# Moving two-input elementwise work of a hybrid decoder kernel from GpSimd to VectorE and ScalarE

## The chip, the cores and the metric

The kernel runs on one core of a Trainium2 chip. The metric is the device time of one execution in microseconds (us). Before the change it is 800.0 us, the median of three runs (799.88 to 800.56).

A core has TensorE for matmuls (PE in the profile; PEld is its loading of weights), VectorE (DVE) and ScalarE (ACT) for elementwise work, GpSimd (POOL), which also does elementwise work, and SyncE (SP), which issues the DMAs here. Each engine works through its own queue in order and waits on semaphores for the others.

## What is computed

Two layers of a decoder with model width 1024 on 256 tokens. Each layer normalises its input, makes one combined projection and feeds three token mixers from it: retention with a rotary embedding (`ret`), attention with a forget gate (`fox`) and an RWKV-7 recurrence (`rwkv`). Their outputs are projected, weighted by sigmoid gates, summed and projected again; then comes a SwiGLU feed-forward part. Cut to what the change touches:

```python
for l in range(DEPTH):
    proj = _rmsnorm(x, mix_norm[l]) @ w_in[l]
    ret_c, fox_c, rwkv_c, gate_c = jnp.split(proj, splits, axis=-1)
    ...
    merged = gates[0] * (y_ret @ p_ret[l]) + gates[1] * (y_fox @ p_fox[l]) + gates[2] * (y_rwkv @ p_rwkv[l])
    x = x + merged @ w_out[l]
    ...
def _rwkv7_branch(cols, mu, ...):
    prev = jnp.pad(cols[:, :-1], ((0, 0), (1, 0), (0, 0)))
    cols = cols + (prev - cols) * mu          # the token mix
    r, k, v, xw, xa, xg = jnp.split(cols, ...)
    ...
    k = k * (1.0 + (a - 1.0) * k_a)           # k2 in the kernel
    y = _rwkv7_scan(r, decay, k, v, -kk, kk * a)
def _rotary(t, pos):
    return jnp.concatenate([t1 * cos - t2 * sin, t1 * sin + t2 * cos], axis=-1)
```

Everything is float32.

## The kernel before

**Layout.** Channels lie on the 128 partitions and the 256 tokens along the free axis. A tile of two channel groups is 128 x 512 elements; most elementwise instructions here have that shape, or half of it (128x256, or 64x512 for half of the partitions).

**Matmuls.** A float32 product is made from three matmuls of rounded parts: weight high by input high, weight high by input low, weight low by input high (L290, L293, L294, in `mm3`; `mm3n` with L437 to L439 has the operands the other way round). The parts of the weights are made on the fly in `_piece`: SyncE loads a raw piece (L263), ScalarE rounds it to `whi` (L273, 128x1024), VectorE subtracts to get `wlo` (L274, 128x1024). Some pieces are made ahead (`AHEAD = 3`, four buffers of each part). So VectorE and ScalarE feed TensorE with weights all the time and do all other elementwise work between the pieces. Inputs of matmuls are split in the same manner by `split`: ScalarE makes `hi` (L376), VectorE or GpSimd makes `lo` (L377).

**Order of the work.** `mixers` starts with the first projections and then runs generators side by side: `gemms` (projections and gates, the long supply of matmuls), `rwkv`, `fox` and `ret`. Each yields a cost out of the table `PACE`, and the one with the smallest sum goes next. That sets the order in which the instructions are written; the order on each engine is then made by a scheduler at build time, which works with priorities (`early`, `high_priority`) and its own estimates of durations, so that an instruction can stand elsewhere in its queue than in the text. On the chip the queues are fixed.

**Buffers.** Most 128x512 tiles come out of one pool, `t2`, with 13 buffers under one tag; a new tile waits until one is free.

**The places that the change touches**, in the order of a layer:

- `rwkv_in` (from L622): the token mix. For each of four pairs of channel groups (r, k, v, and wg for the low-rank inputs) VectorE scales the projection into `pj` (L642), with one column more at the front that GpSimd sets to zero (L640). GpSimd subtracts neighbours into `dd` (L644), and VectorE makes dd * mu + pj (L633, two of 128x256). The multiply-adds of one pair are written after the scaling of the next.
- `rwkv` (from L655): k2 = (scaled a) * k on GpSimd (L730), feeding the second pair of `bk` writes (L732) and rkk (L745), which feeds the matmul pb (L748); two copies of v into `rav` on GpSimd (L735); rs = r-part * decay on GpSimd (L740), read much later (L894); nn = masked part of gg on GpSimd (L786), read by matmuls at L842. Between gg (L764) and L842 stands the inversion of small triangles: gg goes to DRAM and back by DMA into `lt`, a serial solve on VectorE follows (L821, L823), the result goes through DRAM again into `tb`, is transposed (L837) and meets nn at L842.
- `ret` (from L1103): four DMAs make the swapped rows `sw` of the rotary embedding (L1112), two load the cosine and sine tables `cs` (L1114, L1115). GpSimd multiplies qk by the cosine, in place (L1116), VectorE multiplies sw by the sine (L1117) and adds (L1118); the sum feeds the scores psc (L1138), which VectorE masks (L1140, L1141).
- `gemms` (from L529): the merge. With ps the projected branch, VectorE makes (g + 1) * ps (L567) and the sum m += g (L569) runs on GpSimd for all four column groups of the second branch and for the first group (c = 0) of the third; the other three run on VectorE. Of the finished m, hi is made on ScalarE and lo (L377) on GpSimd for c = 0, on VectorE for the others. The output projection, which comes next on TensorE, needs hi and lo of c = 0 first.
- `fox` is not changed; its reduction for the softmax (L1057), its scaling (L1064) and the transposes px (L1068) run beside the `rwkv` steps above.

Of the kernel before, what the change touches and what calls it, by code (L numbers as in the profile page):

```python
# [8 lines left out]
F32 = mybir.dt.float32  # L9
# [4 lines left out]
ALU = mybir.AluOpType  # L14
AX = mybir.AxisListType

P = 128
# [133 lines left out]
class Kernel:  # L151
# [377 lines left out]
    def gemms(self, l, xs, rstd, rn):  # L529
        nc, d = self.nc, self.d  # L530
        fx = []
        self.need = None
        for _ in self.fox_in(l, xs, rn, fx):
            yield PACE["gemms0"]
        self.start.append(("fox", self.fox(l, fx)))
        rt = []
        for _ in self.ret_in(l, xs, rstd, rn, rt):
            yield PACE["gemms1"]
        self.start.append(("ret", self.ret(l, rt)))
        yield PACE["gemms2"]  # L540
        gates = {}
        for b in (0, 1, 2):
            for c in range(4):
                gen = self.gemm_pair(xs)
                while True:
                    try:
                        next(gen)
                    except StopIteration as e:
                        ps = e.value
                        break  # L550
                    yield PACE["gemms3"]
                g = gates[b, c] = self.big.tile([P, 2, T], F32, tag="gate", bufs=8, name=self.nm("gate"))
                nc.vector.tensor_tensor(out=g, in0=ps, in1=self.b2(rstd), op=ALU.mult)  # L553
                nc.scalar.activation(g, g, AF.Tanh, scale=0.5)
                yield PACE["gemms3"]
            if b == 0:
                continue
            for bb in ((0, 1) if b == 1 else (2,)):
                self.need = ("ret", "fox", "rwkv")[bb]
                yield PACE["gemms4"]  # L560
                self.need = None
                y = [(self.y[bb][0][:, k, :], self.y[bb][1][:, k, :]) for k in range(2)]
                for c in range(4):
                    ps = self.run(self.gemm_pair(y))
                    g, m = gates[bb, c], gates[0, c]
                    with self.early("hp_merge"):
                        nc.vector.scalar_tensor_tensor(out=g, in0=g, scalar=1.0, in1=ps, op0=ALU.add, op1=ALU.mult)  # L567
                        if bb:
                            (nc.vector if bb == 2 and c >= 1 else nc.gpsimd).tensor_tensor(out=m, in0=m, in1=g, op=ALU.add)  # L569
                    if bb == 2:  # L570
                        with self.early("hp_turn"):
                            hi, lo = self.split(self.t2, m, [P, 2, T], ("t2", "t2"), nc.gpsimd if c < 1 else nc.vector)
                        self.mx.extend((hi[:, i, :], lo[:, i, :]) for i in range(2))
                    elif c % 2:
                        yield PACE["gemms5"]
# [46 lines left out]
    def rwkv_in(self, l, xs, rstd, first):  # L622
# [5 lines left out]
        wg = self.t512("wg")  # L628
        dst = [r, k, v, wg]

        def mix(j, pj, dd):
            for i in range(2):
                nc.vector.scalar_tensor_tensor(out=dst[j][:, i, :], in0=dd[:, i, :], scalar=self.prm(l, "mu", 2 * j + i),  # L633
                                               in1=pj[:, i, 1:], op0=ALU.mult, op1=ALU.add)

        last = None
        for j in range(4):
            ps = first[j] if j < len(first) else self.run(self.gemm_pair(xs))
            pj = self.big.tile([P, 2, T + 1], F32, tag="pj", bufs=2, name=self.nm("pj"))
            nc.gpsimd.memset(pj[:, :, 0:1], 0.0)  # L640
            for o, p in self.parts(ps):
                nc.vector.tensor_tensor(out=pj[:, o, 1:], in0=p, in1=self.bs(rstd, o), op=ALU.mult)  # L642
            dd = self.t512("dd")
            nc.gpsimd.tensor_tensor(out=dd, in0=pj[:, :, 0:T], in1=pj[:, :, 1:], op=ALU.subtract)  # L644
            if last:
                mix(*last)
            last = j, pj, dd
        mix(*last)
        return r, k, v, wg, rav

    @staticmethod
# [3 lines left out]
    def rwkv(self, l, rw):  # L655
# [71 lines left out]
        k2 = self.t512("k2")  # L727
        for i in range(2):
            nc.scalar.activation(k2[:, i, :], ta[:, i, :], AF.Identity, scale=hb[:, 4 + i:5 + i], bias=hb[:, 6 + i:7 + i])
        nc.gpsimd.tensor_tensor(out=k2, in0=k2, in1=k, op=ALU.mult)  # L730
        for h in range(2):
            nc.vector.tensor_tensor(out=bk[hs[h], :, (1 - h) * C:(2 - h) * C], in0=ch(k2)[hs[h]], in1=ch(pinv)[hs[h]], op=ALU.mult)  # L732
        nc.vector.tensor_tensor(out=rav[:, :, 0:C], in0=ch(r), in1=pp[:, :, 1:], op=ALU.mult)
        for h in range(2):
            nc.gpsimd.tensor_copy(rav[hs[h], :, (2 - h) * C:(3 - h) * C], ch(v)[hs[h]])  # L735
        rs = self.t2.tile([P, 2, NC, C], F32, tag="t2", name=self.nm("rs"))
        r4 = rav.rearrange("p (a c) x -> p a c x", a=2)
        p4 = pp.rearrange("p (a c) x -> p a c x", a=2)
        pend = p4[:, :, 0:NC - 1, C:C + 1].broadcast_to([P, 2, NC - 1, C])
        nc.gpsimd.tensor_tensor(out=rs[:, :, 1:, :], in0=r4[:, :, 1:, 0:C], in1=pend, op=ALU.mult)  # L740
        yield PACE["rwkv5"]

        rkk = self.t512("rkk")
# [39 lines left out]
        nc.gpsimd.memset(tb, 0.0)  # L783
        nn = self.t2.tile([P, NP, C], F32, tag="t2", name=self.nm("nn"))
        for h in range(2):
            nc.gpsimd.tensor_tensor(out=nn[hs[h]], in0=gg[hs[h], h::2, 2 * C:],  # L786
                                    in1=c["nmask"][hs[h]].unsqueeze(1).broadcast_to([64, NP, C]), op=ALU.mult)

        idn = c["ident"]
# [313 lines left out]
    def ret(self, l, rt):  # L1103
# [9 lines left out]
        cs = self.t512("cs")  # L1113
        nc.sync.dma_start(cs[:, 0, :], self.dc("cos"))  # L1114
        nc.sync.dma_start(cs[:, 1, :], self.dc("sin"))  # L1115
        nc.gpsimd.tensor_tensor(out=qk, in0=qk, in1=b4(cs[:, 0, :]), op=ALU.mult)  # L1116
        nc.vector.tensor_tensor(out=sw, in0=sw, in1=b4(cs[:, 1, :]), op=ALU.mult)  # L1117
        nc.vector.tensor_tensor(out=qk, in0=qk, in1=sw, op=ALU.add)  # L1118
        yield PACE["ret0"]
# [77 lines left out]
```

## Time and profile before

| | |
|---|---|
| median of three runs | 800.0 us (799.88 to 800.56) |
| the profiled execution | 800.76 us, of which the span of its instructions is 799.0 |
| busy: PE, PEld | 783.6 us (98%), 762.5 us (95%) |
| busy: DVE, ACT, POOL | 576.2 us (72%), 397.1 us (50%), 61.6 us (8%) |
| instructions on DVE, ACT, POOL | 900, 543, 83 |
| granted TensorE clock | 1.000 |
| HBM | 137 MB read, 173 GB/s over the span |

How to read it: a row of an instruction has the line in the kernel, the engine, the operation, the tile written and those read, shapes, and how many there are. Behind the bar come the busy time in us and the mean of one in ns, then the idle time of the engine just before and what ended it. Rows of a timeline begin with the start and the length in us; in brackets stands the idle time of the engine before the row and what ended it. Since TensorE is busy nearly all the time, idle time on another engine says little; what counts are the waits of TensorE. Spans on GpSimd are rougher than the others.

### The profile page before, as it was taken

The page shows a single profiled execution, that of the slowest core. Times are in us where ns is not written, and L with a number is a line of the kernel's source. Part 1 is how long each engine was busy: PE and PEld are TensorE (multiplying, and loading weights), DVE is VectorE, ACT ScalarE, POOL GpSimd, SP SyncE. Part 2 cuts the span into 40 slices and gives each one's busy share as a digit, 9 for nine tenths or more (in the row PEclk, how much of TensorE's full clock was granted, in tenths as well). Part 3 has the DMA queues.
Part 4 walks back from the last instruction along what each step waited for, and adds up shares of the span by engine and source line. Part 5 has one row for each costly group of instructions (what it writes and reads, how often), then busy time and mean ns, then how long its engine had stood idle before and what let it go on. Part 6 is the DMA issues. An engine that isn't in the chain of part 4 may idle for free.

```text
span 799.0 us, 16543 instructions
## 1 busy us (share of the span) xinstructions
PE 783.6 (98%) x7018; PEld 762.5 (95%) x7018; DVE 576.2 (72%) x900; ACT 397.1 (50%) x543; POOL 61.6 (8%) x83
## 2 busy tenths in 40 slices
PE   8999899999999999999999999999999999999998
PEld 6999899999999999999998988999999999999997
DVE  5897979597867666656678798877878666666453
ACT  6367445535645444445444764554456545444331
POOL 3201210031000000000023030101110000000000
PEclk9999999999999999999999999999999999999999
DMA  8565524335454554556554553452445454555650
GB/s 308 208 226 167 170 80 169 140 114 205 161 208 167 203 205 172 191 184 211 200 188 175 197 172 106 162 174 106 142 176 190 180 201 174 206 202 164 211 190 27
DMA packets 27802, 140.42 MB, mean 176 GB/s; under 512 B 7600, under 2 KB 9168, under 8 KB 12496
## 3 DMA queue, kind: packets, MB, share of 16 engines
q1 hardware_dynamic: 27728, 139.36, 50.2%
q8 instruction: 55, 0.90, 0.5%
q14 instruction: 19, 0.16, 0.1%
HBM read 136.97 MB, written 1.33 MB: 173 GB/s over the span
## 4 chain that ended last, share of the span: by engine, by line
PE 88%; DVE 6%; DMA 2%; ACT 1%; issue 1%; POOL 1%; SPq 0%; POOLq 0%; DVEq 0%; ACTq 0%
PE mm L290 26%; PE mm L294 25%; PE mm L293 25%; DVE wlo L274 2%; PE mqk L439 1%; PE mqk L438 1%; PE mqk L437 1%; ACT whi L273 1%; DMA rsw<-rqk 1%; PE pgm L762 1%; DVE rkk L745 1%; DMA raw<-in_win 1%; DMA raw<-in_pp 1%; PE mv L437 1%; PE mv L439 1%
## 5 line engine op out<-in xcount | busy, mean ns | idle before, releaser
L273 ACT CAST whi<-raw 128x1024 fp32r<-128x1024 f32 (+1 forms) x257 | 264.7, 1033 | 321.7 <-PE mm L293 232.2
L274 DVE TENSOR_TENSOR wlo<-raw,whi 128x1024 fp32r<-128x1024 f32 (+1 forms) x257 | 313.3, 1221 | 143.0 <-ACT whi L273 142.3
L290 PE MATMUL mm<-xh,whi 128*128 128x256 f32 x1312 | 368.0, 280 | 0.5 <-ACT whi L273 0.5
L294 PE MATMUL mm<-xh,wlo 128*128 128x256 f32 x1248 | 346.3, 277 | 0.7 <-DVE wlo L274 0.7
L293 PE MATMUL mm<-xl,whi 128*128 128x256 f32 x1248 | 346.3, 278 | 0.0
L290 PEld LDWEIGHTS mm<-xh,whi 128*128 128x128 f32 x1312 | 246.6, 188 | 2.8 <-issue 0.9
L294 PEld LDWEIGHTS mm<-xh,wlo 128*128 128x128 f32 x1248 | 234.4, 188 | 1.1 <-DVE wlo L274 0.9
L293 PEld LDWEIGHTS mm<-xl,whi 128*128 128x128 f32 x1248 | 234.5, 188 | 0.8 <-issue 0.5
L290 PE MATMUL mm<-hi,whi 128*128 128x256 f32 x576 | 160.1, 279 | 0.0
L294 PE MATMUL mm<-hi,wlo 128*128 128x256 f32 x544 | 150.9, 277 | 0.0
L293 PE MATMUL mm<-lo,whi 128*128 128x256 f32 x544 | 150.8, 277 | 0.0
L290 PEld LDWEIGHTS mm<-hi,whi 128*128 128x128 f32 x576 | 108.2, 188 | 0.6 <-issue 0.3
L294 PEld LDWEIGHTS mm<-hi,wlo 128*128 128x128 f32 x544 | 102.1, 188 | 0.2
L293 PEld LDWEIGHTS mm<-lo,whi 128*128 128x128 f32 x544 | 102.1, 188 | 0.1
L569 POOL TENSOR_TENSOR gate<-gate,gate 128x512 f32<-128x512 f32 x10 | 13.3, 1336 | 142.3 <-DVE gate L567 142.3
L600 DVE TENSOR_TENSOR h<-t,mm 128x512 f32<-128x512 f32 x22 | 15.1, 687 | 11.5 <-PE mm L294 8.6
L567 DVE SCALAR_TENSOR_TENSOR gate<-gate,mm 128x512 f32<-128x512 f32 x24 | 16.1, 682 | 8.6 <-PE mm L294 8.5
L597 DVE TENSOR_TENSOR t<-mm,rstd 128x512 f32<-128x512 f32 (+1 forms) x24 | 15.2, 645 | 8.5 <-PE mm L294 8.5
L553 DVE TENSOR_TENSOR gate<-mm,rstd 128x512 f32<-128x512 f32 x24 | 16.5, 689 | 3.8 <-PE mm L294 3.5
L293 PE MATMUL mm<-xh,wlo 128*128 128x256 f32 x64 | 18.0, 281 | 0.7 <-DVE wlo L274 0.7
L439 PE MATMUL mv<-whi,xl 128*128 128x260 f32 (+1 forms) x64 | 18.6, 290 | 0.0
L437 PE MATMUL mv<-whi,xh 128*128 128x260 f32 (+1 forms) x64 | 18.6, 290 | 0.0
(259 smaller groups left out, 797.9 us busy)
## 6 DMA issues: line engine op xcount, KB each, us to landing
raw<-in_wg SPq DMA_DIRECT2D x44, 1024.0 KB, 4.7
raw<-in_wgate SPq DMA_DIRECT2D x24, 1024.0 KB, 4.8
raw<-in_wd SPq DMA_DIRECT2D x16, 1024.0 KB, 5.0
raw<-in_win SPq DMA_DIRECT2D x13, 1024.0 KB, 8.0
raw<-in_wo SPq DMA_DIRECT2D x8, 1024.0 KB, 4.8
raw<-in_pp SPq DMA_DIRECT2D x6, 1024.0 KB
raw<-in_wd SPq DMA_DIRECT2D x8, 768.0 KB, 4.3
raw<-in_wqk SPq DMA_DIRECT2D x4, 1024.0 KB, 5.0
```

The costliest lines, as they stand in the source:

```text
L273: nc.scalar.copy(hi[:, :m * width], r)
L274: nc.vector.tensor_tensor(out=lo[:, :m * width], in0=r, in1=hi[:, :m * width].bitcast(F32), op=ALU.subtract)
L290: nc.tensor.matmul(out, wh, xh, start=first, stop=False)
L293: nc.tensor.matmul(out, wh, xl, start=False, stop=False)
L294: nc.tensor.matmul(out, wl, xh, start=False, stop=last)
L437: nc.tensor.matmul(out, xh[:, s], wh, start=first, stop=False)
L439: nc.tensor.matmul(out, xl[:, s], wh, start=False, stop=last)
L553: nc.vector.tensor_tensor(out=g, in0=ps, in1=self.b2(rstd), op=ALU.mult)
L567: nc.vector.scalar_tensor_tensor(out=g, in0=g, scalar=1.0, in1=ps, op0=ALU.add, op1=ALU.mult)
L569: (nc.vector if bb == 2 and c >= 1 else nc.gpsimd).tensor_tensor(out=m, in0=m, in1=g, op=ALU.add)
L597: nc.vector.tensor_tensor(out=t[:, o, :], in0=p, in1=self.bs(rstd, o), op=ALU.mult)
L600: nc.vector.tensor_tensor(out=h, in0=t, in1=pu, op=ALU.mult)
```

## The change

All of GpSimd's elementwise work on two inputs goes elsewhere:

- the token mix becomes (1 - mu) * pj on ScalarE, a copy with a scale, and then pj(previous token) * mu + that, one multiply-add on VectorE. The subtraction and its four `dd` tiles a layer are gone, and the multiply-adds of a pair are written right behind its scaling. 1 - mu is made once a layer on GpSimd, 128x8 elements.
- k2, rs, nn, the cosine product, the five merges and the one lo of the merge go to VectorE.
- the two copies of v go to ScalarE.

On GpSimd stay memsets and operations on a few columns of parameters.

```diff
@@ gemms
                         if bb:
-                            (nc.vector if bb == 2 and c >= 1 else nc.gpsimd).tensor_tensor(out=m, in0=m, in1=g, op=ALU.add)
+                            nc.vector.tensor_tensor(out=m, in0=m, in1=g, op=ALU.add)
                     if bb == 2:
                         with self.early("hp_turn"):
-                            hi, lo = self.split(self.t2, m, [P, 2, T], ("t2", "t2"), nc.gpsimd if c < 1 else nc.vector)
+                            hi, lo = self.split(self.t2, m, [P, 2, T], ("t2", "t2"))
@@ rwkv_in
-        def mix(j, pj, dd):
-            for i in range(2):
-                nc.vector.scalar_tensor_tensor(out=dst[j][:, i, :], in0=dd[:, i, :], scalar=self.prm(l, "mu", 2 * j + i),
-                                               in1=pj[:, i, 1:], op0=ALU.mult, op1=ALU.add)
-
-        last = None
+        om = self.sm.tile([P, 8], F32, name="om")
+        nc.gpsimd.tensor_scalar(out=om, in0=self.prm(l, "mu", 0, 8), scalar1=-1.0, scalar2=1.0, op0=ALU.mult, op1=ALU.add)
         for j in range(4):
...
-            dd = self.t512("dd")
-            nc.gpsimd.tensor_tensor(out=dd, in0=pj[:, :, 0:T], in1=pj[:, :, 1:], op=ALU.subtract)
-            if last:
-                mix(*last)
-            last = j, pj, dd
-        mix(*last)
+            for i in range(2):
+                n = 2 * j + i
+                nc.scalar.activation(dst[j][:, i, :], pj[:, i, 1:], AF.Identity, scale=om[:, n:n + 1])
+                nc.vector.scalar_tensor_tensor(out=dst[j][:, i, :], in0=pj[:, i, 0:T], scalar=self.prm(l, "mu", n),
+                                               in1=dst[j][:, i, :], op0=ALU.mult, op1=ALU.add)
@@ rwkv
-        nc.gpsimd.tensor_tensor(out=k2, in0=k2, in1=k, op=ALU.mult)
+        nc.vector.tensor_tensor(out=k2, in0=k2, in1=k, op=ALU.mult)
...
-            nc.gpsimd.tensor_copy(rav[hs[h], :, (2 - h) * C:(3 - h) * C], ch(v)[hs[h]])
+            nc.scalar.copy(rav[hs[h], :, (2 - h) * C:(3 - h) * C], ch(v)[hs[h]])
...
-        nc.gpsimd.tensor_tensor(out=rs[:, :, 1:, :], in0=r4[:, :, 1:, 0:C], in1=pend, op=ALU.mult)
+        nc.vector.tensor_tensor(out=rs[:, :, 1:, :], in0=r4[:, :, 1:, 0:C], in1=pend, op=ALU.mult)
...
-            nc.gpsimd.tensor_tensor(out=nn[hs[h]], in0=gg[hs[h], h::2, 2 * C:],
+            nc.vector.tensor_tensor(out=nn[hs[h]], in0=gg[hs[h], h::2, 2 * C:],
@@ ret
-        nc.gpsimd.tensor_tensor(out=qk, in0=qk, in1=b4(cs[:, 0, :]), op=ALU.mult)
+        nc.vector.tensor_tensor(out=qk, in0=qk, in1=b4(cs[:, 0, :]), op=ALU.mult)
```

## The prediction

> **What bounds the kernel now.** I read the page first, then TensorE's waits, then the stretches of 20 us around them, and last the timelines of VectorE, GpSimd and TensorE at the two longest waits.
>
> ```profile
> PE 783.6 (98%) x7018; PEld 762.5 (95%) x7018; DVE 576.2 (72%) x900; ACT 397.1 (50%) x543; POOL 61.6 (8%) x83
> ```
>
> TensorE is busy for 98% of the span. No engine that the change touches can give more than the 15 us in which TensorE is idle, and part of that is start and tail. So the question is which idle time of TensorE ends on GpSimd or on a VectorE that GpSimd holds up.
>
> ```profile
> PE mm L294 <- POOL lo L377: 3.1, 2, 1.6
> PE pb L748 <- DVE rkk L745: 2.9, 2, 1.5
> PE px L1068 <- DVE lg L1064: 1.5, 2, 0.7
> ...
> PE pn L842 <- DVE dn L837: 0.2, 1, 0.2
> ```
>
> The columns are total us, times, longest us. The first line is GpSimd itself, once in each layer. The next two stand behind VectorE, again once in each layer. Together they are 7.5 us. The last line is small, but it ends a long chain that comes up among the rivals.
>
> ```profile
> 20.00:40.00 20.00, 20.00 (x147) 18.87 (x147) 16.92 (x32) 7.39 (x8) 4.26 (x6) 1.00 0.58 206
> ...
> 80.00:100.00 20.00, 17.80 (x144) 16.52 (x143) 19.49 (x26) 9.41 (x20) 4.61 (x3) 1.00 0.53 168
> 100.00:120.00 20.00, 19.84 (x189) 18.66 (x189) 15.45 (x36) 8.40 (x13) 3.19 (x3) 1.00 0.29 82
> ```
>
> After the length the columns are PE, PEld, DVE, ACT, POOL, then the granted clock. Between 80 and 100 us VectorE is busy 19.49 of 20 and TensorE only 17.80: there VectorE is the bound. In the token mix (20 to 40) TensorE has no gap, and from 100 on VectorE has 4.5 us to spare.
>
> Is VectorE's 19.49 all work? These are VectorE's and then GpSimd's rows of the same microseconds, and two instructions over both layers (minimum, median, maximum in ns):
>
> ```profile
> 79.38 2.38 DVE L725 SCALAR_TENSOR_TENSOR bk<-ka,pinv 64x512 f32<-64x512 f32 x2
> ...
> 84.31 3.00 DVE L745 SCALAR_TENSOR_TENSOR rkk<-r,par,k 128x256 f32<-128x256 f32 x2
> ```
> ```profile
> 79.30 1.91 POOL L730 TENSOR_TENSOR k<-k,k 128x512 f32<-128x512 f32 x1 [7.47 <-ACT k L729]
> 84.18 2.45 POOL L1116 TENSOR_TENSOR rqk<-rqk,cs 128x1024 f32<-128x1024 f32 x1 [2.98 <-DMA cs<-in_const]
> ```
> ```profile
> L725 DVE SCALAR_TENSOR_TENSOR bk<-ka,pinv x4: 673/1182/1691, 79.4 to 471.8; 64x512 f32<-64x512 f32 x4
> ```
> ```profile
> L745 DVE SCALAR_TENSOR_TENSOR rkk<-r,par,k x4: 471/1536/2608, 84.3 to 478.6; 128x256 f32<-128x256 f32 x4
> ```
>
> The same instruction on the same shape takes 0.47 us or 2.61. The long one starts at 84.31, just after GpSimd's L1116 (84.18 to 86.63), and is over soon after it. It is the same with L725 beside L730: 0.67 us becomes 1.69. So VectorE with two SBUF inputs stands still while GpSimd reads: 1.02 + 2.14 = 3.2 us of the 19.49 are not work.
>
> **The change part by part.** Durations come from the profiled execution (span 799.0 us, 1.76 us around it: 800.76); the median of the runs is 800.0, so I take the gains off 800.0, and a profiled execution would show 0.76 more. The prices of the moved instructions on their new engines, from the nearest rows:
>
> ```profile
> L713 DVE TENSOR_TENSOR kkr<-kkr,pss x2: 686/688/689, 75.0 to 466.7; 128x512 f32<-128x512 f32 x2
> ```
> ```profile
> L1117 DVE TENSOR_TENSOR rsw<-rsw,cs x2: 1220/1220/1220, 96.0 to 487.8; 128x1024 f32<-128x1024 f32 x2
> ```
> ```profile
> L392 ACT ACTIVATE xh<-x,par x32: 492/504/513, 4.6 to 614.7; 128x256 fp32r<-128x256 f32 x32
> ```
> ```profile
> L1036 ACT COPY ka<-pqk x4: 580/581/582, 70.9 to 463.2; 64x512 f32<-64x512 f32 x4
> ```
> ```profile
> L569 POOL TENSOR_TENSOR gate<-gate,gate 128x512 f32<-128x512 f32 x10 | 13.3, 1336 | 142.3 <-DVE gate L567 142.3
> L644 POOL TENSOR_TENSOR dd<-pj 128x512 f32<-128x512 f32 x8 | 8.7, 1094 | 35.2 <-DVE pj L642 35.2
> ...
> L740 POOL TENSOR_TENSOR rs<-rav,pdec 128x384 f32<-128x384 f32 x2 | 3.6, 1788 | 55.7 <-DVE u L351 55.7
> ```
>
> VectorE takes over in each layer: five merges (L569) at 0.69, one remainder (L377) at 0.69, k2 at 0.69, two halves of nn (64x512 each) at 0.69, rs at 0.55 (estimate: three quarters of 0.69 and a little) and the cosine product at 1.22, together 7.9 us. ScalarE takes over eight scaled copies at 0.50 and two copies of v at 0.58, together 5.2 us.
>
> *Token mix, from 30 us.* The subtraction on GpSimd goes (four of 1.1 us a layer). The eight multiply-adds on VectorE stay as many and as wide, and they too were held:
>
> ```profile
> L633 DVE SCALAR_TENSOR_TENSOR r<-dd,par,pj x4: 473/860/1245, 32.3 to 425.2; 128x256 f32<-128x256 f32 x4
> ```
>
> VectorE gains about 0.77 us on one of r's two, and I take the same for k and v: 2.3 a layer. But TensorE is busy 20.00 of 20 here, so this is worth nothing; 0 is my value. ScalarE is busy 7.39 of 20, so its eight copies fit. What is new is a wait: each multiply-add now stands behind a scaled copy on ScalarE's queue, and behind it on VectorE the weight remainders (L274) that feed TensorE. If VectorE stands for every copy, that is 8 x 0.5 = 4 us a layer against the 2.3 gained, and 1.7 late. The weight pieces made ahead cover a part or all of it; I keep 0 to 1.7 us of loss a layer for the range. Four fewer buffers of the 13 in the shared pool are taken; that can only let others start earlier. The new 128x8 operation for 1 - mu runs on an idle GpSimd before the data is there: nothing.
>
> *k2, rs and the cosine product, 75 to 101 us.* Ahead of rkk VectorE loses 3.2 us of standing still and gains k2, 0.69. The cosine product needs a table by DMA; its sister L1117, which needs the same table and the swapped rows, ran only at 96.0. I place the cosine product beside it, behind rkk. Then rkk is done 3.2 - 0.7 = 2.5 us earlier, more than TensorE's wait for it (1.5), which goes.
>
> ```profile
> 87.36 1.12 PE L748 MATMUL pb<-rkk,con 128*128 128x512 f32 x2 [1.46 <-DVE rkk L745]
> ...
> 91.10 0.65 PE L1068 MATMUL px<-con,lg 128*128 128x128 f32 x4 [0.74 <-DVE lg L1064]
> ```
>
> Next late is lg for px: TensorE would be there 1.46 us earlier, lg (there at about 91.0, when the wait ends) 2.5 earlier; that wait of 0.74 goes too. 1.46 + 0.74 = 2.2. Then VectorE pays the cosine product, 1.22, and stands only 1.3 us ahead of its old time:
>
> ```profile
> L1138 PE MATMUL psc<-rqk x16: 376/394/480, 100.9 to 497.8; 64*128 64x256 f32 x16
> L1118 DVE TENSOR_TENSOR rqk<-rqk,rsw x2: 1216/1216/1217, 97.8 to 489.5; 128x1024 f32<-128x1024 f32 x2
> ```
>
> L1118 ends at 99.0, 1.9 us before psc. With TensorE 2.2 earlier and VectorE 1.3, 1.0 us of that slack is left, so the scores do not wait. Weight pieces might. The gain lies between VectorE's own 1.3 and TensorE's 2.2; I take 1.7 us a layer, the middle, because VectorE has room right behind. If cosine product and rs both land ahead of rkk, 3.2 - 0.7 - 1.2 - 0.5 leaves 0.8: that is the low end.
>
> *nn, from 107 us.* Two instructions, 1.4 us, go onto VectorE where it is idle 4.5 us in 20 (100:120). It is read only at L842, after the solve: 0, and 1.4 if that cover is gone.
>
> *Merge and its first remainder, 192 to 204 us.*
>
> ```profile
> 192.00:206.00 14.00, 12.45 (x108) 12.25 (x107) 11.38 (x15) 6.64 (x9) 3.51 (x3) 1.00 0.47 170
> ```
> ```profile
> 197.43 2.09 POOL L377 TENSOR_TENSOR lo<-gate,hi 128x512 fp32r<-128x512 f32 x1 [0.73 <-ACT hi L376]
> ```
> ```profile
> 195.88 1.36 DVE L569 TENSOR_TENSOR gate<-gate,gate 128x512 f32<-128x512 f32 x1
> 197.17 1.21 DVE L274 TENSOR_TENSOR wlo<-raw,whi 128x1024 fp32r<-128x1024 f32 x1
> ...
> 202.44 1.28 DVE L377 TENSOR_TENSOR lo<-gate,hi 128x512 fp32r<-128x512 f32 x2
> ```
> ```profile
> 199.57 0.39 PE L294 MATMUL mm<-lo,whi 128*128 128x256 f32 x1 [1.55 <-POOL lo L377]
> ...
> 204.63 0.28 PE L294 MATMUL mm<-lo,whi 128*128 128x256 f32 x1
> ```
>
> It is tempting to book the whole 1.55. But VectorE is busy 11.38 us of the 11.7 up to 203.7. It loses 0.67 of standing still (1.36 against 0.69) and takes two instructions that cost 0.64 each in a row (1.28 for two): 0.6 later at the last remainder, 204.3 instead of 203.7. The matmul of that remainder ran at 204.63. So if the order on VectorE stays, the wait at the first remainder turns into one at the last and the gain is 0.3; if weight remainders (1.21 each, at 197.17 and elsewhere) fall behind, it is the whole 1.55; if one more falls ahead, it is a loss of 0.9. I take 0.5, near the low row.
>
> The other four merges come earlier; TensorE's waits name neither them nor what they hold up: 0.
>
> Sum: 1.7 + 0.5 = 2.2 a layer, 4.4 us. 800.0 - 4.4 = **795.6 us**. With the ends of the two places (0.8 to 2.2, -0.9 to 1.55) it is 2 x -0.1 to 2 x 3.75, that is 800.2 to 792.5, and with the whole loss in the token mix 803.6; I expect most of it between 793 and 798.
>
> **The rivals.** *VectorE becomes the bound (slower).* TensorE's own supply, the weight remainders, comes from VectorE, which is full at 80 to 100 and at 192 to 204. If k2, cosine product, rs and nn all fall among the rows up to 108 us, 0.69 + 1.22 + 0.55 + 1.38 = 3.8 us is added against 3.2 freed: 0.6 later; the merge adds 0.6 more. 1.2 a layer, 2.4 in all: 802.4. It decides once more than 3.2 us of moved work stands ahead of what TensorE waits for. For it: VectorE's 19.49 of 20. Against it: nn has gaps from 100 on, and the freed time is certain wherever a GpSimd row overlaps. Chance 0.13.
> [...]
>
> *The stretching has another cause.* Then nothing is freed; VectorE's additions before TensorE's waits cost 1.9 + 1.3 a layer, 806.4. Against it: 0.47 beside 2.61 us for one instruction, each time beside GpSimd. Chance 0.04.
>
> *The gain is given back (no change).* From gg (L764) a chain through DMAs and a serial solve leads to L842, where TensorE already waits a little (0.2). If that chain does not move up with TensorE, the 1.7 of each layer returns as a wait there and 0.5 stays: 799.0. Against it: gg is fed by TensorE itself and moves with it. Chance 0.16.
>
> *All waits go.* A new order that puts the remainders first gives 2.2 + 1.55 a layer: 800.0 - 7.5 = 792.5, and perhaps 1 us more where other matmuls wait on a shorter VectorE queue: 791.5. It needs the order to be lucky twice. Chance 0.12.
>
> **How the numbers follow.** The forecast has 0.55. Over 0.2% is over 1.6 us, about what a measurement of this kernel can tell from no change. Faster: 0.55 + 0.12 = 0.67; same 0.16; slower 0.13 + 0.04 = 0.17. The range takes in the case that all waits go, and of the slower ones those up to 1.5 us over the time before: 791.0 to 801.5 leaves out about 0.18, nearly all of it above. The likeliest case alone spans 793 to 798.
>
> **What would show it.** Right: no VectorE instruction over its usual length beside GpSimd (L745 at 0.47, L725 at 0.67 throughout); TensorE's waits lose pb and the GpSimd line; a shorter wait behind a VectorE remainder (L377) takes its place; VectorE's busy time hardly rises although its 22 more instructions are worth 16 us; ScalarE's rises by about 10. Wrong: a wait of TensorE for wlo (L274) between 30 and 110 us, a VectorE row waiting for ScalarE in the token mix, the cosine product ahead of rkk, or a longer wait at L842.

## The result and the profile after

The kernel after takes 807.24 us (median of 4 runs, 805.75 to 808.31), the kernel before 800.24 (4 runs, 799.88 to 800.56): a ratio of 1.0089, 95% interval 1.0076 to 1.0102. The change makes it slower by 7 us. The prediction said faster, 795.6. The profiled execution of after took 806.63 us, its span is 804.8. In the runs below three executions were disturbed, of e1 the profiled one (2748.86 us), of e7 one (870.74) and of the kernel before one (2743.66): the ratios leave them out, and without them the medians of e1 and e7 are 809.30 and 806.71 us.

The page of after, first TensorE's share, then its waits (total us, times, longest us):

```profile
PE 791.4 (98%) x7018; PEld 766.7 (95%) x7018; DVE 570.0 (71%) x922; ACT 404.4 (50%) x563; POOL 15.1 (2%) x51
```

```profile
PE mm L294 <- DVE lo L377: 4.0, 2, 2.0
PE mm L290 <- DVE gate L567: 1.4, 2, 0.7
...
PE pn L837 <- DVE dn L832: 0.3, 2, 0.2
...
PE px L1063 <- DVE lg L1059: 0.2, 1, 0.2
```

The wait for GpSimd and the one for rkk are gone, that for lg nearly. VectorE has 22 instructions more and is busy 6.2 us less. (From the token mix on, a line has a number lower by 5 than before.) But a wait of 2.0 us a layer behind VectorE's remainder stands where 1.55 stood behind GpSimd's, with 0.7 ahead of it. And TensorE has the same 7018 matmuls and is "busy" 7.8 us longer. That is the line to be suspicious of: the same work can't be more work.

The stretch from 80 to 100 us of after (PE, PEld, DVE, ACT, POOL, granted clock), and rkk, which GpSimd had held up most:

```profile
80.00:100.00 20.00, 19.91 (x162) 18.46 (x160) 18.12 (x27) 10.14 (x20) 0.95 (x1) 1.00 0.49 161
```

```profile
L740 DVE SCALAR_TENSOR_TENSOR rkk<-r,par,k x4: 479/480/480, 83.8 to 479.3; 128x256 f32<-128x256 f32 x4
```

rkk takes 0.48 us each time (before: up to 2.61), and from 80 to 100 us TensorE is busy 19.91 instead of 17.80. That half came as forecast.

Now the merge in the first layer: VectorE's timeline, and TensorE's.

```profile
195.39 0.69 DVE L569 TENSOR_TENSOR gate<-gate,gate 128x512 f32<-128x512 f32 x1
196.00 0.68 DVE L567 SCALAR_TENSOR_TENSOR gate<-gate,mm 128x512 f32<-128x512 f32 x1
196.59 1.22 DVE L274 TENSOR_TENSOR wlo<-raw,whi 128x1024 fp32r<-128x1024 f32 x1
197.73 0.69 DVE L569 TENSOR_TENSOR gate<-gate,gate 128x512 f32<-128x512 f32 x1
198.33 1.27 DVE L567 SCALAR_TENSOR_TENSOR gate<-gate,mm 128x512 f32<-128x512 f32 x2
199.53 1.28 DVE L569 TENSOR_TENSOR gate<-gate,gate 128x512 f32<-128x512 f32 x2
200.73 0.68 DVE L377 TENSOR_TENSOR lo<-gate,hi 128x512 fp32r<-128x512 f32 x1
```

```profile
199.06 0.38 PE L290 MATMUL mm<-hi,whi 128*128 128x256 f32 x1 [0.70 <-DVE gate L567]
201.47 0.58 PE L294 MATMUL mm<-lo,whi 128*128 128x256 f32 x1 [2.02 <-DVE lo L377]
...
202.49 0.41 PE L290 MATMUL mm<-hi,whi 128*128 128x256 f32 x1
202.70 0.41 PE L293 MATMUL mm<-hi,wlo 128*128 128x256 f32 x1
```

The first column group is summed at 196.1 (first row), but its remainder starts at 200.73, behind one weight remainder, and the products (L567) and sums of all three later groups. The merge is raised in priority (`hp_merge` is 44), the remainder is not (`hp_turn` is 0). On GpSimd that did not matter: there the remainder started at 197.43, as soon as its hi was there. And after the wait a matmul starts every 0.21 us (202.49, 202.70), until 204.6, where the usual distance is 0.12. Two windows of 3.41 us, ahead of that and in it:

```profile
197.86:201.27 3.41, 0.88 (x6) 0.49 (x4) 3.41 (x6) 2.59 (x4) 0.00 (x0) 1.00 0.32 132
201.27:204.68 3.41, 3.21 (x15) 3.21 (x16) 3.08 (x5) 0.19 (x1) 0.11 (x1) 0.50 0.30 55
```

The granted clock is 0.50 for 3.41 us, and 15 matmuls fit where 31 fit in before (the row is shown with experiment e7). TensorE counts as busy all the same (3.21 of 3.41 us). That is a part of the 7.8 us: in e3, whose clock stays at 1.00, TensorE is busy 788.3 us, so about 3.1 go with the two slow stretches. The other 4.7 have another cause, which shows at e8.

Where the time went is read best from marks that both kernels pass. The table has the start of a matmul in TensorE's timeline, less its start in before's: the first pm (139.4 us in before; the gain of 75 to 101 us is in by then), pu (behind the solve), pv (180.9, end of the recurrence), and the last pn (227.2, the norm behind the merge); then the same in the second layer. All are from one profiled execution each.

| kernel | pm | pu | pv | pn | pm, layer 2 | pv | pn and end |
|---|---|---|---|---|---|---|---|
| after | -2.06 | +6.34 | +0.11 | +2.94 | +1.35 | +3.03 | +5.85 |
| e2 cosine only | -1.64 | +6.75 | +0.07 | +0.06 | -2.09 | -0.82 | -1.06 |
| e3 after, remainder first | -1.57 | +6.82 | +0.60 | +0.06 | -1.38 | +0.31 | -0.21 |
| e4 after, cosine on GpSimd | -0.05 | -0.03 | +1.02 | +3.93 | +2.77 | +3.97 | +5.27 |
| e5 first group only | +0.56 | +0.37 | +0.36 | +3.18 | +2.99 | +3.38 | +4.62 |
| e6 second branch only | -0.18 | -0.03 | +1.02 | +0.71 | +0.52 | +1.58 | +1.28 |
| e7 remainder twice | -0.30 | -0.05 | -0.05 | +1.49 | +1.30 | +1.66 | +4.80 |
| e8 order restored | -1.63 | -0.80 | -0.81 | -1.35 | -2.94 | -2.09 | -2.60 |
| e9 the rest of the change | -0.32 | -0.33 | -0.32 | -0.58 | -0.56 | -0.28 | -0.53 |
| e10 raise undone | -1.44 | +6.96 | +0.27 | -0.19 | -1.63 | -0.39 | -0.83 |

Read after's row by differences. The stage of 75 to 101 us gains 1.6 us a layer (-2.06 less the 0.41 that after has at 28 us already; 1.35 - 2.94). The 0.41 is scatter of one execution: e3, e4, e8, e9 and e10, which have the same token mix, lie between -0.21 and +0.10 at the first pl (74 us). From pm to pv 2.2 and 1.7 are lost again. From pv to pn, the merge, 2.83 and 2.82 are lost.

### The profile page after: what moved, and what is told of

Same layout as the page of the kernel before. It is cut to its first block, busy times and chain, and to the rows that moved or that the text cites. A ratio compares the mean times of both kernels' runs of the same rounds, so it can differ in the third digit from the quotient of the medians.

```text
span 804.8 us, 16533 instructions
## 1 busy us (share of the span) xinstructions
PE 791.4 (98%) x7018; PEld 766.7 (95%) x7018; DVE 570.0 (71%) x922; ACT 404.4 (50%) x563; POOL 15.1 (2%) x51
## 4 chain that ended last, share of the span: by engine, by line
PE 89%; DVE 5%; DMA 2%; ACT 1%; issue 1%; SPq 0%; DVEq 0%; ACTq 0%
PE mm L294 25%; PE mm L290 25%; PE mm L293 25%; DVE wlo L274 2%; PE mqk L439 1%; PE mqk L438 1%; PE mqk L437 1%; ACT whi L273 1%; PE mv L437 1%; PE pgm L757 1%; PE mv L438 1%; PE mv L439 1%; DVE gate L567 1%; DMA rsw<-rqk 1%; DMA raw<-in_win 1%
## 5 line engine op out<-in xcount | busy, mean ns | idle before, releaser
L274 DVE TENSOR_TENSOR wlo<-raw,whi 128x1024 fp32r<-128x1024 f32 (+1 forms) x257 | 308.8, 1203 | 151.0 <-ACT whi L273 150.0
L290 PE MATMUL mm<-xh,whi 128*128 128x256 f32 x1312 | 367.7, 280 | 0.4 <-ACT xh L392 0.4
L294 PE MATMUL mm<-xh,wlo 128*128 128x256 f32 x1248 | 346.6, 278 | 0.8 <-DVE wlo L274 0.8
L293 PE MATMUL mm<-xl,whi 128*128 128x256 f32 x1248 | 346.1, 277 | 0.0
L290 PEld LDWEIGHTS mm<-xh,whi 128*128 128x128 f32 x1312 | 246.5, 188 | 2.5 <-issue 0.9
L294 PEld LDWEIGHTS mm<-xh,wlo 128*128 128x128 f32 x1248 | 234.4, 188 | 1.7 <-DVE wlo L274 1.0
L290 PE MATMUL mm<-hi,whi 128*128 128x256 f32 x576 | 161.3, 280 | 1.4 <-DVE gate L567 1.4
L294 PE MATMUL mm<-hi,wlo 128*128 128x256 f32 x544 | 151.6, 279 | 0.0
L290 PEld LDWEIGHTS mm<-hi,whi 128*128 128x128 f32 x576 | 109.6, 190 | 2.4 <-DVE gate L567 1.8
L294 PEld LDWEIGHTS mm<-hi,wlo 128*128 128x128 f32 x544 | 102.4, 188 | 0.3
L439 PE MATMUL mv<-whi,xl 128*128 128x260 f32 (+1 forms) x64 | 18.6, 290 | 0.0
L437 PE MATMUL mv<-whi,xh 128*128 128x260 f32 (+1 forms) x64 | 18.5, 290 | 0.0
L438 PE MATMUL mv<-wlo,xh 128*128 128x260 f32 (+1 forms) x64 | 18.4, 287 | 0.0
L294 PE MATMUL mm<-xl,whi 128*128 128x256 f32 x64 | 17.8, 280 | 0.3 <-DVE xl L393 0.3
```

Source lines behind the costliest of these rows:

```text
L274: nc.vector.tensor_tensor(out=lo[:, :m * width], in0=r, in1=hi[:, :m * width].bitcast(F32), op=ALU.subtract)
L290: nc.tensor.matmul(out, wh, xh, start=first, stop=False)
L293: nc.tensor.matmul(out, wh, xl, start=False, stop=False)
L294: nc.tensor.matmul(out, wl, xh, start=False, stop=last)
L437: nc.tensor.matmul(out, xh[:, s], wh, start=first, stop=False)
L438: nc.tensor.matmul(out, xh[:, s], wl, start=False, stop=False)
```

## The experiments

Theory Q after the result: what costs is the place that moved instructions get in the queues, first of all that of the first remainder. The rival D, by which that place is not the cause, is priced in each expectation of the first four.

**e1: the merges alone.** Before with all five merges and the remainder on VectorE.

```diff
-(nc.vector if bb == 2 and c >= 1 else nc.gpsimd).tensor_tensor(out=m, in0=m, in1=g, op=ALU.add)
+nc.vector.tensor_tensor(out=m, in0=m, in1=g, op=ALU.add)
-hi, lo = self.split(self.t2, m, [P, 2, T], ("t2", "t2"), nc.gpsimd if c < 1 else nc.vector)
+hi, lo = self.split(self.t2, m, [P, 2, T], ("t2", "t2"))
```

> The kernel before with only the merge moved: the five sums (L569) and the one remainder (L377) on VectorE. Theory Q (queue and clock): the first remainder stands on VectorE behind the merges of the other column groups, which carry a raised priority, TensorE idles more than 2 us just there, the granted clock falls to 0.5 for 3.4 us, and each layer loses about 2.8 us: 805 to 807 us. Theory D (VectorE has too much to do, and the loss goes with the us moved onto it): the moved instructions cost 4.1 us a layer and about 4 us of standing still beside GpSimd go, so 800 to 801.5 us, with no stretch of half clock.

Measured: 809.45 us against 800.13, ratio 1.0100 (1.0073 to 1.0126). The merges alone cost all that the change costs; Q's number is missed by more than 2 us, D's by about 8. The times of this kernel's profile can't be compared, so it has no row in the table, but VectorE's order is that of after: the first remainder stands behind the sums of all three later groups.

**e2: the cosine product alone.**

```diff
-nc.gpsimd.tensor_tensor(out=qk, in0=qk, in1=b4(cs[:, 0, :]), op=ALU.mult)
+nc.vector.tensor_tensor(out=qk, in0=qk, in1=b4(cs[:, 0, :]), op=ALU.mult)
```

> The kernel before with only the cosine product (L1116) on VectorE. Theory Q: rkk (L745) falls to 0.47 us and TensorE gains 1 to 1.6 us a layer up to the masked products, but the order made at build time now puts the small matmuls behind the triangular solve some 65 large matmuls later and close together, where their waits show, and about 2 us a layer are lost there: 800.5 to 802.5 us. Theory D: 1.2 us is added and 2.1 us freed a layer, so it is faster: 797 to 798.5 us.

Measured: 799.60 us against 800.13, ratio 0.9984 (0.9974 to 0.9994), between the two expectations. By pm this one line has the whole gain of after (-1.64). Then pu is 6.75 us late and at pv nothing is left (+0.07), just as in after. So one line brings both the gain and what takes it back. In the second layer not all goes: of 2.15 us gained by pm, 0.88 are left at pv.

SyncE's queue shows the second. Before, after, and the kernel of e8 further down (start us, length, row):

```profile
130.35 1.14 SPq L827 DMA_DIRECT2D d<-ti  x2
...
132.87 4.26 SPq L832 DMA_DIRECT2D tb<-d  x8
```

```profile
135.99 1.13 SPq L822 DMA_DIRECT2D d<-ti  x2
139.72 0.34 SPq L263 DMA_DIRECT2D raw<-in_wgate  x1
141.35 4.90 SPq L827 DMA_DIRECT2D tb<-d  x8
```

```profile
132.74 1.14 SPq L823 DMA_DIRECT2D d<-ti  x2
135.27 3.65 SPq L828 DMA_DIRECT2D tb<-d  x8
```

The result of the solve leaves at 135.99 instead of 130.35, and the way back at 141.35 instead of 132.87, behind a weight load that waits for its buffer. That is the order fixed at build time: on VectorE 50 instructions stand between the first and the last step of the solve in after, 49 in e2 and 43 in before, and on TensorE pu stands behind 953 large matmuls (L290 to L294, L437 to L439) in after and e2, behind 888 in before. What follows up to py stays in front of the same 984th, squeezed together.

**e3: after, with the remainder raised like the merge.**

```diff
-'hp_merge': 44.0, 'hp_turn': 0.0
+'hp_merge': 44.0, 'hp_turn': 44.0
```

> The changed kernel with the priority of the remainders of the merge raised to that of the merges (hp_turn 0 to 44); the work on each engine is the same. Theory Q: the first remainder runs about 2.5 us earlier, TensorE's wait for it falls from 2.0 us to under 0.7, the clock stays at 1.0, and the merge costs 3 to 4 us a layer less: 799 to 801.5 us. Theory D: VectorE's work is the same, the wait only moves to a later remainder: 805 to 807 us.

Measured: 801.31 us against 800.13, ratio 1.0016 (1.0004 to 1.0029): 5.9 of the 7 us are back by one number in a table. From VectorE's and TensorE's timelines of e3:

```profile
198.22 0.69 DVE L377 TENSOR_TENSOR lo<-gate,hi 128x512 fp32r<-128x512 f32 x1
```

```profile
198.96 0.39 PE L294 MATMUL mm<-lo,whi 128*128 128x256 f32 x1 [0.23 <-DVE lo L377]
```

The remainder runs at 198.22 instead of 200.73 and TensorE waits 0.23 us for it. From pv to pn e3 gains 0.54 us on before (0.60 to 0.06), where after lost 2.83. That is the forecast's 0.5 for this place, reached with the remainder first. D is out.

**e4: after, with the cosine product back on GpSimd.**

```diff
-nc.vector.tensor_tensor(out=qk, in0=qk, in1=b4(cs[:, 0, :]), op=ALU.mult)
+nc.gpsimd.tensor_tensor(out=qk, in0=qk, in1=b4(cs[:, 0, :]), op=ALU.mult)
```

> The changed kernel with only the cosine product back on GpSimd. Theory Q: the order behind the solve is that of the kernel before again and the 2 us a layer lost there come back, but rkk is held by GpSimd again for 2 us and TensorE's gain ahead of it goes down by 1 to 1.5 us a layer; the merge stays bad: 804.5 to 806.5 us. Theory D: VectorE has 1.2 us a layer less to do but stands still 2.1 us more: 807 to 809 us.

Measured: 807.67 us against 800.13, ratio 1.0097 (1.0068 to 1.0126). That lies in D's range and 1.2 us over Q's; of the four executions two lie in Q's range (806.04, 806.16) and two above D's (809.19, 809.72), so the number decides nothing. The row in the table goes against D's reason: in the first layer the gain is gone at pm and pu is in its old place, as Q had it, but there is a new loss at pv, +1.02. So there was a third cause that neither theory had. In the second layer 1.16 us of gain stay, where Q had them gone: pb does not wait for rkk there, since rkk (479.88) starts ahead of GpSimd's cosine product (480.35).

**e5: the first group alone.** Before, with only the merge and the remainder of the third branch's first group on VectorE.

```diff
-(nc.vector if bb == 2 and c >= 1 else nc.gpsimd).tensor_tensor(out=m, in0=m, in1=g, op=ALU.add)
+(nc.vector if bb == 2 else nc.gpsimd).tensor_tensor(out=m, in0=m, in1=g, op=ALU.add)
-hi, lo = self.split(self.t2, m, [P, 2, T], ("t2", "t2"), nc.gpsimd if c < 1 else nc.vector)
+hi, lo = self.split(self.t2, m, [P, 2, T], ("t2", "t2"))
```

> Before, with one edit: the first column group of the third branch has its merge and its remainder on VectorE; all other work as before. Theory Q (the first remainder queues behind the raised merges of the later column groups, and the longer wait ends in a half-rate clock): 2.8 us a layer, 805 to 807, and in the profile one stretch of about 3.4 us at granted clock 0.5 behind each of two waits of 2 us for lo. Rival C (the loss of the merges alone comes mostly from the merges of the second branch): 800 to 802.

Measured: 805.39 us against 800.14, ratio 1.0065 (1.0041 to 1.0089), Q's number. Two moved instructions a layer cost 5 us. But in the profile only one of the two waits ended in a slow clock, where Q had both: in the first layer pv to pn lost 2.82 us, in the second 1.24, with the same wait for lo (4.0 us in two). These are its windows, PE busy first, the clock behind POOL:

```profile
199.38:202.79 3.41, 1.39 (x10) 1.19 (x11) 3.41 (x6) 1.54 (x3) 0.00 (x0) 1.00 0.02 5
202.79:206.20 3.41, 3.41 (x19) 3.41 (x18) 1.82 (x4) 0.00 (x0) 0.11 (x1) 0.50 0.66 211
591.91:595.33 3.42, 2.33 (x19) 1.94 (x17) 3.42 (x6) 1.89 (x3) 0.00 (x0) 1.00 0.68 278
595.33:598.74 3.41, 1.76 (x15) 1.77 (x16) 3.41 (x6) 1.22 (x2) 0.00 (x0) 1.00 0.00 0
```

So the wait costs 1.24 us a layer, and a slow stretch, where there is one, 1.58 more. e4 has the same waits (4.0 us in two) and bears this out: pv to pn loses 2.91 us in its first layer and 1.30 in its second, and the mean granted clock of its profiled execution, 0.998, is by estimate that of one slow stretch in a span of 804.3 us (0.5 x 3.41 us lost).

**e6: the second branch's merges alone.**

```diff
-(nc.vector if bb == 2 and c >= 1 else nc.gpsimd).tensor_tensor(out=m, in0=m, in1=g, op=ALU.add)
+(nc.vector if bb == 1 or c >= 1 else nc.gpsimd).tensor_tensor(out=m, in0=m, in1=g, op=ALU.add)
```

> Before, with one edit: the four merges of the second branch on VectorE, the third branch as before. Theory C (they stand in VectorE's queue inside the recurrence of us and S): the last pS 2 us later a layer, pv 1.0 to 2.0 later, 802 to 804. Rival Q (only the queue before the first remainder matters): 799.5 to 800.8.

Measured: 801.98 us against 800.14, ratio 1.0021 (1.0012 to 1.0030). That is C's mechanism, at the lower end of its range: pv is 1.0 us late in each layer, and the norm behind it gets 0.3 back. VectorE's timeline of e6 shows how:

```profile
166.52 0.28 DVE L914 SCALAR_TENSOR_TENSOR us<-us,pdec 128x64 f32<-128x64 f32 x1
166.72 0.68 DVE L569 TENSOR_TENSOR gate<-gate,gate 128x512 f32<-128x512 f32 x1
167.33 0.69 DVE L567 SCALAR_TENSOR_TENSOR gate<-gate,mm 128x512 f32<-128x512 f32 x1
167.94 0.21 DVE L917 TENSOR_TENSOR S<-us,pS 128x64 f32<-128x64 f32 x1
```

The recurrence is a chain of small steps (L914, L917) with matmuls pS between them. Raised merges of 0.68 us now stand between its links, and the last pS moves from 167.7 to 170.0. On GpSimd the sums waited in a queue of their own and nobody asked for them. e5 and e6 together cost 7.1 us, e1 9.3 with an interval from 5.8 to 10.1.

**e7: the longer wait by itself.** Before, with GpSimd's remainder computed twice: 2.09 us more on GpSimd, no work moved.

```diff
-(engine or nc.vector).tensor_tensor(out=lo, in0=src, in1=hf, op=ALU.subtract)
+for _ in range(2 if engine is nc.gpsimd else 1):
+    (engine or nc.vector).tensor_tensor(out=lo, in0=src, in1=hf, op=ALU.subtract)
```

> Before, with GpSimd computing the remainder of the first column group twice (2.09 us more, same values), so that TensorE's wait there grows from 1.55 to 3.6 us and nothing else moves. Theory G (a longer stop of TensorE makes the granted clock fall to 0.5 for 3.4 us, which costs another 1.5 us): 3.6 us a layer, 806.5 to 808, with two stretches at clock 0.50. Rival W (the clock fell for a reason of the changed kernel, not for the wait): 2.1 us a layer, 804 to 804.8, clock 1.0.

Measured: 807.07 us against 800.14, ratio 1.0077 (1.0060 to 1.0094), G's number. TensorE's wait is 3.33 us in the first layer, 1.78 more than before's. Windows of e7 and of before, PE busy first:

```profile
196.05:199.47 3.42, 1.92 (x17) 1.72 (x16) 3.42 (x5) 2.12 (x3) 2.69 (x2) 1.00 0.73 295
199.47:202.88 3.41, 1.57 (x13) 1.58 (x14) 3.41 (x5) 1.24 (x2) 1.70 (x1) 1.00 0.00 0
202.88:206.29 3.41, 3.41 (x32) 3.41 (x31) 1.87 (x3) 0.00 (x0) 0.11 (x1) 1.00 0.51 139
592.00:595.41 3.41, 0.16 (x1) 0.16 (x2) 3.41 (x5) 1.36 (x2) 3.12 (x2) 1.00 0.19 79
595.41:598.82 3.41, 3.41 (x17) 3.41 (x18) 3.28 (x5) 0.62 (x1) 0.00 (x0) 0.50 0.15 19
```

```profile
197.77:201.18 3.41, 1.86 (x16) 1.66 (x15) 3.41 (x6) 2.04 (x4) 1.75 (x1) 1.00 0.34 137
201.18:204.60 3.42, 3.42 (x31) 3.42 (x30) 2.54 (x4) 0.26 (x1) 0.11 (x1) 1.00 0.25 60
```

In the first layer the clock is 1.00 in all three rows, also behind the wait, which ends at 201.31: the merge loses 1.54 us. In the second TensorE is busy 0.16 us of the 3.41 from 592.00, and the clock of the next 3.41 is 0.50: the merge loses 3.14. The difference, 1.60, agrees with e5's 1.58. Why the clock fell in one layer and not in the other no run shows. W is out: the slow clock comes behind a longer wait also in a kernel that has nothing of the change.

**e8: the order restored.** After with three edits: e3's; the steps of the solve raised, so that they keep their place; the second branch's merges back on GpSimd.

```diff
-'hp_turn': 0.0
+'hp_turn': 44.0
...
-nc.vector.tensor_tensor(out=m, in0=m, in1=g, op=ALU.add)
+(nc.vector if bb == 2 else nc.gpsimd).tensor_tensor(out=m, in0=m, in1=g, op=ALU.add)
...
+with self.tc.high_priority(100):
     nc.vector.tensor_tensor(out=tmp[:, :, 0:n], ...)
     nc.vector.tensor_reduce(out=ti[:, :, i], in_=tmp[:, :, 0:n], axis=AX.X, op=ALU.add)
```

> After, with three edits: the remainder raised as the merges are (44), the 14 steps of the solve raised by 100 so that they keep the place they had before, and the second branch's merges back on GpSimd. If the gain of 75 to 101 us (1.65 us a layer) is lost only through the late solve and the merges: 1.65 plus 0.5 a layer and 0.4 at the start, 795 to 796.5. Rival R (the gain is given back at the next bound whatever the order): 799 to 800.5.

Measured: 799.21 us against 800.14, ratio 0.9988 (0.9978 to 0.9997). It is faster than both kernels, than after by 8 us, though no faster than e2 by the ratios. But the number is R's, and the first expectation failed: half of the 1.63 us at pm is lost by pv (-0.81), although pu stands behind 888 large matmuls again. In the first layer no wait of TensorE explains that: between 75 and 182 us before stands still for 2.35 us in gaps of over 0.1, e8 for 0.17. The order does. TensorE's timeline, before and then e8, pm and the two groups of pn behind it:

```profile
139.40 0.97 PE L814 MATMUL pm<-uw,gg 64*64 64x64 f32 x26
...
140.34 1.11 PE L842 MATMUL pn<-dn,nn 64*64 64x64 f32 x30
...
144.41 1.15 PE L849 MATMUL pn<-tb,vn 64*64 64x64 f32 x32
```

```profile
137.77 1.15 PE L809 MATMUL pm<-uw,gg 64*64 64x64 f32 x32
...
139.40 0.32 PE L838 MATMUL pn<-dn,nn 64*64 64x64 f32 x2
...
141.50 1.14 PE L838 MATMUL pn<-dn,nn 64*64 64x64 f32 x30
...
143.61 1.15 PE L845 MATMUL pn<-tb,vn 64*64 64x64 f32 x32
```

From the first pm to the start of the second pn both run the same 88 matmuls, 32 pm, 32 pn and 24 large ones. Before runs pm and the first pn as one block and takes 5.01 us. In e8 the large ones stand in between, as 3, 14 and 7, and it takes 5.84: the 0.83 that is lost.

The same had happened ahead of pm. The large matmul that starts at 92.94 us in before starts at 90.74 in e8, 2.2 us earlier, with the waits for rkk and lg behind it; the one of 110.83 starts at 109.34, only 1.5 earlier. Between them:

```profile
108.60 1.09 PE L797 MATMUL ptr<-con,rav 128*128 128x128 f32 x8
```

```profile
106.88 1.00 PE L792 MATMUL ptr<-con,rav 128*128 128x128 f32 x6
107.80 0.43 PE L1142 MATMUL pyr<-rsc,rv 128*64 128x128 f32 x2
...
108.39 0.44 PE L792 MATMUL ptr<-con,rav 128*128 128x128 f32 x2
```

In before eight ptr run as one group of 1.09 us; in e8 the new order breaks them into six and two with pyr between: 1.00 and 0.44. So R's number came by the order, at two more places. No run puts these groups together again; that this alone would bring back the 0.7 and the 0.8 is read from the rows and not tested.

**e9: the rest of the change.** After, with the cosine product, the merges and the remainder as before; the token mix, k2, rs, nn and the copies of v stay moved.

```diff
-nc.vector.tensor_tensor(out=m, in0=m, in1=g, op=ALU.add)
+(nc.vector if bb == 2 and c >= 1 else nc.gpsimd).tensor_tensor(out=m, in0=m, in1=g, op=ALU.add)
-hi, lo = self.split(self.t2, m, [P, 2, T], ("t2", "t2"))
+hi, lo = self.split(self.t2, m, [P, 2, T], ("t2", "t2"), nc.gpsimd if c < 1 else nc.vector)
-nc.vector.tensor_tensor(out=qk, in0=qk, in1=b4(cs[:, 0, :]), op=ALU.mult)
+nc.gpsimd.tensor_tensor(out=qk, in0=qk, in1=b4(cs[:, 0, :]), op=ALU.mult)
```

> After, with the cosine product, the merges and the first remainder as before: what is left of the change is the token mix, k2, rs, nn and the copy of v. Theory N (none of these lies on the path that sets the end): 799.6 to 800.6, TensorE's waits as before, pb behind rkk still there. Rival T (the token mix or nn gains or loses by itself): under 799.2 or over 801.

Measured: 799.95 us against 800.04, ratio 0.9994 (0.9985 to 1.0004): nothing that can be measured. TensorE's waits in e9:

```profile
PE mm L294 <- POOL lo L377: 3.1, 2, 1.5
PE pb L743 <- DVE rkk L740: 2.8, 2, 1.4
PE px L1063 <- DVE lg L1059: 1.2, 2, 0.6
```

They are before's, nearly. The token mix, k2, rs, nn and the copies of v together change nothing, although they are all of ScalarE's new work and a third of VectorE's (2.6 of 8.0 us a layer).

**e10: e8 without the raise of the solve.**

```diff
-with self.tc.high_priority(100):
```

> The kernel of e8 without the raise of the solve's steps, so that TensorE's matmuls behind the solve stand 65 large matmuls later again. Theory S (the late solve costs 0.8 to 1.3 us a layer): 800.8 to 801.8, pu 6 us late in the profile. Rival C (what e8 has over e3 comes from the second branch's merges alone): 799.0 to 799.6.

Measured: 800.01 us against 800.04, ratio 0.9997 (0.9988 to 1.0007), between the two. pu is late again (+6.96), and from pm to pv e10 loses 1.71 and 1.24 us where e8 loses 0.82 and 0.85: the late solve costs 0.89 us in the first layer, within S's price, and 0.39 in the second, below it. Against e3 (2.17 and 1.69) the second branch's merges are worth 0.46 and 0.45 here. So both seem to have a part. But these are differences of single executions: e5, e7 and e9, which keep before's order from pm to pv, differ from before there by -0.20 to +0.25 us in the first layer and by +0.28 to +0.39 in the second.

## Why the prediction was wrong, point by point

With these runs after's two layers can be added up. First layer: 0.41 gained at the start, by scatter, and 1.65 by pm; lost: 0.82 to the order at pm and pn (e8), 0.89 to the late solve (e10 less e8), 0.46 to the second branch's merges (e3 less e10), 1.24 to the first remainder's wait and 1.58 to the slow clock (both e5): +2.93, measured 2.94. Second layer: -1.59 + 0.85 + 0.39 + 0.45 + 1.24 + 1.58 = +2.92, measured 2.91. From pm to pv this is no proof, since the three terms add up to e3's loss (2.17 and 1.69) however it is divided, and e3 has after's order there. In the merge it is one: e5's 1.24 + 1.58 = 2.82 meets after's 2.83 and 2.82.

- **What bounds the kernel, and what held VectorE up: right.** Neither of the two VectorE rows is stretched any more (in after L740 takes 0.48 us throughout, L720 0.67 to 0.69), and VectorE's busy time fell by 6.2 us, where the prediction had it hardly rise: more was freed than the rows of L745 and L725 had shown. The longest L274 went from 2.27 us to 1.31. The stretching is measured row by row and is no rule for two SBUF inputs: in before the L274 of 163.92 us took 2.25 beside GpSimd's L569, the one of 197.17 its usual 1.21 beside GpSimd's L377.
- **Token mix, k2, rs, nn at nothing: right**, by e9. ScalarE's busy time rose by 7.3 us, not 10.
- **75 to 101 us: right in mechanism; the size has luck in it.** The two waits go as summed: the large matmul of 92.94 us in before starts 2.24 us earlier in after, with the 0.41 of the start taken off, where 1.46 + 0.74 gave 2.2. The forecast then went down to 1.7 because VectorE pays the cosine product. 1.65 and 1.59 are left at pm, but because pyr and ptr were broken up, as in e8; no wait for VectorE stands there. e2 shows that the cosine product alone does it. It ran behind rkk (93.4 us in the first layer), as placed. (The moved work on VectorE adds up to 8.0 us a layer, not 7.9.)
- **The step that failed first is the one for the merge and its first remainder.** "If the order on VectorE stays" was the condition, and 0.5 of gain the value, with a loss of 0.9 as the end "if one more falls ahead". Not one more but three sums, three products (L567) and a weight remainder fell ahead. The diff itself showed it: the merge is written under `hp_merge`, the remainder under `hp_turn`, and moving both into the one queue where they compete makes that difference count. Instead of a gain of 0.5 it was a loss of 1.24 a layer, and of 1.6 for the clock, for which the prediction had no term at all. e5 has both, e3 undoes both.
- **The second that failed is the argument against "the gain is given back".** That rival had the right place (the solve up to L842) and the wrong reason: the data didn't come too late, the instructions were written later. "gg is fed by TensorE itself and moves with it" holds for data; the order in the queues is made at build time, and one instruction of 1.22 us moved pu by 65 large matmuls. The wait at L842 (L837 in after) hardly grew, 0.2 to 0.3: the delay by order did not show as a wait.
- **"The other four merges come earlier: 0" failed too.** They came earlier, and stood in the recurrence's way: 1.0 us a layer at pv by themselves (e6), by the marks 0.45 in after's order. That nobody waits for an instruction does not say that nobody waits behind it.
- The rival "VectorE becomes the bound" had the right sign and not the cause: VectorE is not fuller than before (18.12 of 20 us from 80 to 100, 19.49 before). One L569 takes 1.34 us on GpSimd and 0.69 on VectorE, and yet e5 and e6, which move it, are 5.3 and 1.8 us slower.

## What to carry to other kernels

Before an instruction moves to another engine, ask what stands ahead of it in the new queue and what will stand behind it, by the priorities under which each is written; a slower engine with an empty queue can be the better place (e5: 5.3 us). Where queues are ordered at build time, compare the order of both programs away from the edit too, since a single move can reorder a stage 50 us later, and such a loss showed here as late marks (pu 6.75 us late in e2), hardly as a wait (0.5 us in two at L842). When a busy bottleneck engine gets busier with the same instructions, look at its clock (0.50 for 3.41 us twice in after), and at groups of small instructions that a new order has broken up.

## What the runs showed of the hardware

The clock was not expected. Behind TensorE's waits at the merge the granted clock was 0.50 for 3.41 us in both layers of after, in the first of e5 and in the second of e7; in the 3.41 us just ahead TensorE was busy 0.88, 0.98, 1.39 and 0.16 us. Across the same wait it was 1.00 in the second layer of e5 (591.91 to 598.74 us) and in the first of e7 (196.05 to 206.29), and in before across the shorter one (197.77 to 204.60). The second of after's layers:

```profile
593.80:597.22 3.42, 0.98 (x6) 0.79 (x7) 3.42 (x6) 2.02 (x4) 0.00 (x0) 1.00 0.08 34
597.22:600.63 3.41, 3.41 (x19) 3.41 (x18) 2.29 (x4) 0.00 (x0) 0.11 (x1) 0.50 0.51 161
```

So the same wait in the same program cost 1.6 us more in one layer than in the other (e5, e7); what decides between the two no run shows. A kernel with such a wait varied from run to run: e5's five took from 802.69 us at a mean clock of 1.000 (before and two waits of 1.24 are 802.6) to 808.05 at 0.992, after's four from 805.75 at 0.998 to 808.31 at 0.994.
